# An RWKV-7 branch inside a two-layer trunk: per-layer state steps for all head pairs at once, small-tile matmul groups emitted whole, 64-row operands padded to 128 rows

## The chip, the cores and the metric

The kernel runs on one core of one Trainium2 chip. The metric is the device time of one execution in microseconds (us), less is better. Engines are named as the profile names them: PE is the matmul engine (TensorE), PEld its weight loads, DVE VectorE, ACT ScalarE, POOL GpSimd, SP SyncE, whose queue issues nearly all DMAs.

## The reference, cut to what matters

512 tokens of width 2048 go through two layers. Each layer normalises x, projects it with `w_in`, feeds three branches (an mLSTM with 4 heads, an attention with 8 heads, an RWKV-7 with 8 heads of 64), gates and concatenates them and projects back with `w_out`. The change lies in the RWKV branch:

```python
def rwkv7_scan(r, w, k, v, a_vec, b_vec):
    def step(S, inp):
        rt, wt, kt, vt, at, bt = inp
        sa = jnp.einsum('bhvk,bhk->bhv', S, at)
        S = S * wt[:, :, None, :] + sa[..., None] * bt[:, :, None, :] + vt[..., None] * kt[:, :, None, :]
        return S, jnp.einsum('bhvk,bhk->bhv', S, rt)
...
    log_w = -jax.nn.softplus(-(w0 + jnp.tanh(xw) @ w2)) - 0.5
    a = jax.nn.sigmoid(a0 + xa @ a2)
    if vres is None: v_first = v
    else: v = v + (v_first - v) * jax.nn.sigmoid(v0 + (v @ v1) @ v2)
    ...
    y = rwkv7_scan(r_h, heads(decay), k_h, v_h, -kk, kk * a_h)
    y = head_layer_norm(y, ln_g, ln_b, RW_GN_EPS)
    y = y + jnp.sum(r_h * k_h * r_k, axis=-1, keepdims=True) * v_h
```

## The kernel before

**The big products.** `gemm` computes 256 columns of `h @ w_in` per call, as 4 weight tiles of 512 KB. Each value is split into two fp32r parts, so a product is three passes (line 235; line 231 for `mv`, token-major). The outputs are called `pg_rk`, `pg_mq` and so on after the columns; all have 128 contracted rows and fill the whole array. Weight tiles come over SP as `raw_*` (lines 319, 324) and are split by ACT (`whi_*`, line 146) and DVE (`wlo_*`, line 147). Results are parked in DRAM and fetched again. `w_out` is the same in `out_products` (`po`, line 1347).

**The RWKV branch** is worked in chunks of 64 tokens, two heads (a pair) at a time on 128 partitions, 4 pairs a layer. `rw_pair(p)` is a generator that yields between its steps:

1. decay and gate: `psw`, `psa` (lines 710 to 714). Each adds a high part on 128 rows and a low part that lies in 64 rows of the tile `wal`.
2. keys: `kk`, `kh`, `bk` (on POOL, line 760), `ar`; then `psG` (line 773): per chunk and head one matmul with 64 rows, 128 columns of weights and 128 moving columns, for two heads in two banks, in two halves of 4 chunks.
3. `psTk` transposes (line 803), then the inverse of a 64x64 triangular matrix: 16x16 blocks on DVE between two DRAM round trips (`inv_d`), then 32x32 tiles on PE: `psQ`, `psT`, `psQ` again (`psQ64`), `psX` (lines 866, 887, 895).
4. `v` (with its correction in layer 1), its transposes, `psR` (line 798), `psW` (line 933, 64x64 tiles), then `psN` and `psY` (lines 798 and 954, 128 rows, 64 columns) and `psM` (line 933).
5. the state: for chunks 1 to 7 in turn, two `psY` matmuls that add to the output (line 960), two `psS` matmuls (line 964) and one DVE step that makes the next S (line 966).
6. norm over the heads, transposes `psTy`, gate, store to `mix_d`.

**What sets the order.** The program is written as generators that `bg.along(ratio, main, side, every)` interleaves: for each step of `main` it emits `ratio` steps of the big products, and every `every` steps one of `side`. Pairs 0 to 2 run their steps 5 and 6 beside steps 1 and 2 of the next pair; pair 3 runs them beside `ml_head(0)` and `ml_head(1)`. The compiled program is not in that order: the tile context places each engine's instructions by a simulated timeline, so that single matmuls of the big products land between small ones wherever a bank or an operand isn't ready. An fp32 matmul of the program is two records in the trace, an fp32r matmul one.

**Banks and buffers.** Two PSUM banks have the tag `bank`, two `bank2`, three `gbank` (big products), one `bank3`. `psG` and `prod2` took theirs from `bank` alone. The tag `tmp` has four buffers of 256 KB.

Of the kernel before, what the change touches and what calls it, by code (L numbers as in the profile page):

```python
# [12 lines left out]
F32 = mybir.dt.float32  # L13
# [9 lines left out]
T = 512  # L23
# [4 lines left out]
R_HEADS, R_ATT = 0.8, 0.0  # L28
# [45 lines left out]
def trunk(ctx, tc, a, out):  # L74
# [6 lines left out]
    dma = nc.sync.dma_start  # L81

# [430 lines left out]
    for l in range(DEPTH):  # L513
# [27 lines left out]
        def misc_out(u, ps, l=l):  # L541
            if u == 0:
                wa = stage(f"wa{l}")
                shift(wa, normed(stage(f"wn{l}"), ps), 12)
                act(wa[0:64], wa[0:64], AF.Tanh)

                kept["wa"] = whh, ahh, wal = [rp.tile([128, T], F32R, name=f"{n}{l}") for n in ("whh", "ahh", "wal")]
                for m, own in ((whh, slice(0, 64)), (ahh, slice(64, 128))):
                    for r in (0, 64):
                        act(m[r:r + 64], wa[own], AF.Copy)  # L550
                    tt(wal[own], wa[own], m[own].bitcast(F32), ALU.subtract)
                return
# [104 lines left out]
        xp_ctx = ExitStack()  # L657
        xp = xp_ctx.enter_context(tc.tile_pool(name=f"xp{l}", bufs=1, side="left"))
# [21 lines left out]
        def rw_pair(p, l=l):  # L680
# [4 lines left out]
            whh, ahh, wal = kept["wa"]  # L685

            tailp, tails, tbank = (xp, ("late", 3), bank2) if p < 3 else (rp, ("tmp", 4), bank)

            def late(name):
                return tailp.tile([128, T], F32, tag=tails[0], bufs=tails[1], name=f"{name}{nm}")  # L690
# [23 lines left out]
            mm(psa, lhsT=a2[64:128, sl], rhs=wal[64:128], start=False, stop=True)  # L714
# [38 lines left out]
            bv = tailp.tile([128, T], F32, tag="bv", bufs=2 if p < 3 else 1, name=f"bv{nm}")  # L753
            nc.scalar.copy(bv, ps)

            hs = [slice(0, 64), slice(64, 128)]
            bk = rp.tile([128, 8, 2, 64], F32, tag="bk", name=f"bk{nm}")
            for h, q in enumerate(hs):
                for slot, x in ((h, kk), (1 - h, kh)):
                    nc.gpsimd.tensor_tensor(bk[q, :, slot, :], x[q].rearrange(c64, t=64), Ei[q].rearrange(c64, t=64), ALU.mult)  # L760

            yield "keys"
            GG = rp.tile([128, 2, 8, 192], F32, tag="GG", name=f"GG{nm}")
            wide = tmp("wide").rearrange("p (c t) -> p c t", t=64)
            marb = mar.rearrange("p a t -> p (a t)")
            for half in range(2):
                cs = slice(half * 4, half * 4 + 4)
                pv = [bank(f"psG{half}{h}{nm}").rearrange("p (c n) -> p c n", n=128) for h in range(2)]  # L770
                for c in range(4):
                    for h, q in enumerate(hs):
                        mm(pv[h][:, c, :], lhsT=bk[q, half * 4 + c].rearrange("p s t -> p (s t)"),
                           rhs=ar[q, :, half * 4 + c, :], start=True, stop=True)
                for h in range(2):
                    tt(GG[:, h, cs, 0:128], pv[h], marb[:, None, :].broadcast_to([128, 4, 128]), ALU.mult)
                yield

            def token_major(blocks, dst, nn):

                ps = bank(f"psT{nn}{nm}")
# [11 lines left out]
            def prod(lhs, rhs, name):  # L793

                pv = bank(f"{name}{nm}").rearrange("p (c n) -> p c n", n=64)
                for c in range(8):
                    for h, q in enumerate(hs):
                        mm(pv[q, c, :], lhsT=lhs(h, c), rhs=rhs(h, c), start=True, stop=True)
                return pv
# [7 lines left out]
            yield  # L807

# [12 lines left out]
            both = small([64, 2, 512], "AR", "TX")  # L821
# [37 lines left out]
            flip()  # L859

# [11 lines left out]
            tt(Q, prod32(lambda q, c, n: GG[q, n // 2, c, n % 2 * 32:n % 2 * 32 + 32], blk(T32), "psQ"),  # L872
               mq.rearrange("p a b -> p (a b)")[:, None, :].broadcast_to([128, 8, 32]), ALU.mult)
# [15 lines left out]
            for h in range(2):  # L889
                nc.scalar.copy(Q[q4[2 * h + 1]], pv[q4[2 * h + 1]])  # L890
            ps = bank(f"psX64{nm}")
            pv = ps[:, 0:256].rearrange("p (c n) -> p c n", n=32)
            for c in range(8):
                for h in range(2):
                    mm(pv[q4[2 * h], c, :], lhsT=Q[q4[2 * h + 1], c, :], rhs=X32[q4[2 * h + 1], c, :],
                       start=True, stop=True)
# [5 lines left out]
            v = fetch("rv")  # L902
            if l > 0:
                bg.ensure("rv1")
                ps = bank(f"psv2_{nm}")
                mm(ps, lhsT=v2[:, p * 128:(p + 1) * 128], rhs=kept["vv"], start=True, stop=True)
                yield
                s = tmp("vs")
                sigm(s, ps, pch(R_V0 + p))
                vf = tmp("vf")  # L910
                dma(vf, vf_d[p])
                tt(vf, vf, v, ALU.subtract)
                tt(vf, vf, s, ALU.mult)
                tt(v, v, vf, ALU.add)
            tt(bv, bv, v, ALU.mult)

            UV = rp.tile([128, 2, 8, 64], F32, tag="UV", name=f"UV{nm}")
            token_major(lambda tb: v[:, tb * 128:(tb + 1) * 128], lambda h: UV[hs[1 - h], h], "v")
            yield
            AR = small([128, 8, 128], "AR")  # L920
            token_major(lambda tb: ar[:, 0, 2 * tb:2 * tb + 2, :].rearrange("p c n -> p (c n)"),
                        lambda h: AR[hs[h], :, 0:64], "a")
            nc.scalar.copy(AR[:, :, 64:128], prod(lambda h, c: GG[hs[1 - h], h, c, 0:64],
                                                  lambda h, c: UV[hs[1 - h], h, c, :], "psR"))
            yield

            def prod2(lhs, rhs, name):

                for half in range(2):
                    pv = bank(f"{name}{half}{nm}").rearrange("p (c n) -> p c n", n=128)  # L930
                    for c in range(4):
                        for h, q in enumerate(hs):
                            mm(pv[q, c, :], lhsT=lhs(h, half * 4 + c), rhs=rhs(h, half * 4 + c), start=True, stop=True)
                    yield slice(half * 4, half * 4 + 4), pv
            Wm = small([128, 8, 64], "Wm")
            for cs, pv in prod2(lambda h, c: X[hs[h], c, :], lambda h, c: AR[hs[h], c, :], "psW"):
# [3 lines left out]
                yield  # L940
            MT, Yl, DN = [late(n).rearrange("p (c n) -> p c n", n=64) for n in ("MT", "Yl", "DN")]
            dc = tailp.tile([128, 8], F32, tag="dc", bufs=2, name=f"dc{nm}")
            nc.vector.tensor_copy(dc, E[:, :, 64])
            tt(DN, prod(lambda h, c: GG[:, h, c, 128:192], lambda h, c: UV[:, h, c, :], "psN"),
               dc[:, :, None].broadcast_to([128, 8, 64]), ALU.mult)
            yield
            for cs, pv in prod2(lambda h, c: Wm[hs[h], c, :], lambda h, c: GG[hs[h], h, c, 64:192], "psM"):
# [3 lines left out]
            psY = tbank(f"psY{nm}").rearrange("p (c n) -> p c n", n=64)  # L951
            for c in range(8):
                for h, q in enumerate(hs):
                    mm(psY[q, c, :], lhsT=GG[:, h, c, 64:128], rhs=UV[:, h, c, :], start=(c == 0), stop=(c == 0),
                       skip_group_check=True)
            yield "state"
            S = DN[:, 0, :]
            for c in range(1, 8):
                for q in hs:
                    mm(psY[q, c, :], lhsT=Yl[q, c, :], rhs=S[q], start=False, stop=True, skip_group_check=True)  # L960
                if c < 7:
                    psS = tbank(f"psS{nm}_{c}")[:, 0:64]
                    for q in hs:
                        mm(psS[q], lhsT=MT[q, c, :], rhs=S[q], start=True, stop=True)
                    S2 = rp.tile([128, 64], F32, tag="S", bufs=2, name=f"S{nm}_{c}")
                    stt(S2, psS, dc[:, c:c + 1], DN[:, c, :], ALU.mult, ALU.add)
                    S = S2
                    if c % 2 == 0:
                        yield
            Y = late("Y").rearrange("p (c n) -> p c n", n=64)  # L970
            nc.scalar.copy(Y, psY)


            st = rp.tile([128, 2, 8], F32, tag="st", name=f"st{nm}")

            def c8(m):
                return m[:, :, None].broadcast_to([128, 8, 64])
            nc.vector.tensor_reduce(st[:, 0, :], Y, AX.X, ALU.add)
            tsc(st[:, 0, :], st[:, 0, :], 1.0 / 64, None, ALU.mult)
            tt(Y, Y, c8(st[:, 0, :]), ALU.subtract)  # L980
            sq = late("ysq")
# [516 lines left out]
```

## Time and profile before

| | |
|---|---|
| median of 3 runs | 2037.14 us (2032.81, 2037.14, 2037.67) |
| the profiled execution: time, span | 2034.48 us, 2032.8 us |
| mean granted PE clock | 0.997 of full |
| DVE busy | 1226.3 us (60%), 2127 instructions |
| ACT busy | 844.2 us (42%), 1435 instructions |
| DMA | 252.27 MB, 124 GB/s in the mean |

The span is the time from the first to the last instruction that the profiler saw; the time of the same execution is 1.7 us longer. A PE that is shown busy may still wait inside that time: matmul ends are modelled, so distances between starts say more than durations.

### The profile page before, as it was taken

The numbers are of one execution on the slowest core, as the hardware profiler recorded it, in microseconds if no ns is written. First come the engines' busy times: TensorE is split into PE (matmuls) and PEld (weight loads), VectorE is DVE, ScalarE is ACT, GpSimd is POOL, SyncE is SP. The second block draws the span as 40 slices with busy tenths as digits, with TensorE's granted clock in tenths as the row PEclk, the third lists the DMA queues.
The fourth block names the chain that finished last, engine by engine and source line by source line (L and its number), as shares of the span: only waits on it lengthen the run. The fifth ranks groups of instructions, "written<-read, shape, count | busy, mean of one in ns | idle before, by whom it ended". The sixth has DMA issues, their size and how long they took to land.

```text
span 2032.8 us, 31556 instructions
## 1 busy us (share of the span) xinstructions
PE 1998.6 (98%) x12544; PEld 1644.6 (81%) x12544; DVE 1226.3 (60%) x2127; ACT 844.2 (42%) x1435; POOL 137.2 (7%) x168
## 2 busy tenths in 40 slices
PE   8999999999999999999999999999999999899998
PEld 6887787888778888888888777877978888787886
DVE  6764766667646578633366547647657657885333
ACT  6523334244425446422263234234334445664223
POOL 3000101001000021000001001001010000210000
PEclk9999999999999999999999999999999999999999
DMA  5442443424445543344444333434424435533334
GB/s 170 140 125 86 118 120 99 120 84 133 116 128 161 169 117 97 114 145 132 131 114 137 110 109 105 120 104 119 125 75 137 142 118 172 147 113 121 121 118 155
DMA packets 239481, 252.27 MB, mean 124 GB/s; under 512 B 49204, under 2 KB 177406, under 8 KB 239334
## 3 DMA queue, kind: packets, MB, share of 16 engines
q1 hardware_dynamic: 238486, 249.29, 40.5%
q8 instruction: 98, 1.61, 0.3%
q0 software_dynamic: 848, 0.97, 0.2%
q14 instruction: 49, 0.40, 0.1%
HBM read 206.16 MB, written 44.06 MB: 123 GB/s over the span
## 4 chain that ended last, share of the span: by engine, by line
PE 91%; DVE 3%; DMA 2%; ACT 2%; issue 1%; SPq 0%; POOL 0%; ACTq 0%; DVEq 0%
PE po L1347 17%; PE pg_az L235 7%; PE pg_mv L231 5%; PE pg_rr L235 4%; PE pg_mq L235 4%; PE pg_rz L235 4%; PE pg_cq L235 4%; PE pg_mk L235 4%; PE pg_rk L235 4%; PE pg_rv L235 4%; PE pg_mo L235 4%; PE pg_mz L235 4%; PE pssc L1268 2%; PE pg_misc L235 2%; PE pg_ck L235 2%; PE psqn L1205 2%
## 5 line engine op out<-in xcount | busy, mean ns | idle before, releaser
L1347 PE MATMUL po<-whi_o,mh 128*128 128x512 f32 x512 | 200.3, 391 | 0.1
L1347 PE MATMUL po<-whi_o,ml 128*128 128x512 f32 x512 | 199.3, 389 | 0.0
L147 DVE TENSOR_TENSOR wlo_o<-raw_o,whi_o 128x1024 fp32r<-128x1024 f32 x64 | 78.3, 1225 | 188.6 <-ACT whi_o L146 187.4
L1347 PE MATMUL po<-wlo_o,mh 128*128 128x512 f32 x512 | 187.7, 390 | 0.0
L146 ACT ACTIVATE whi_o<-raw_o 128x1024 fp32r<-128x1024 f32 x64 | 67.7, 1059 | 204.2 <-PE po L1347 168.6
L1347 PEld LDWEIGHTS po<-whi_o,mh 128*128 128x128 f32 x512 | 96.2, 188 | 20.4 <-DVE Vl L250 0.6
L1347 PEld LDWEIGHTS po<-wlo_o,mh 128*128 128x128 f32 x512 | 96.0, 188 | 20.0
L1347 PEld LDWEIGHTS po<-whi_o,ml 128*128 128x128 f32 x512 | 96.1, 188 | 19.6
L235 PE MATMUL pg_az<-xl,whi_az 128*128 128x512 f32 x256 | 100.8, 394 | 0.0
L235 PE MATMUL pg_az<-xh,whi_az 128*128 128x512 f32 x256 | 100.8, 394 | 0.0
L235 PE MATMUL pg_az<-xh,wlo_az 128*128 128x512 f32 x256 | 100.0, 394 | 0.0
L760 POOL TENSOR_TENSOR bk<-kk,Ei 64x512 f32<-64x512 f32 x16 | 25.8, 1614 | 817.2 <-DVE E L721 476.0
L231 PE MATMUL pg_mv<-whi_mv,xl 128*128 128x256 f32 x256 | 73.2, 286 | 0.0
L231 PE MATMUL pg_mv<-whi_mv,xh 128*128 128x256 f32 x256 | 73.0, 285 | 0.0
L231 PE MATMUL pg_mv<-wlo_mv,xh 128*128 128x256 f32 x256 | 72.7, 285 | 0.0
L235 PEld LDWEIGHTS pg_az<-xl,whi_az 128*128 128x128 f32 x256 | 48.1, 188 | 9.5
L235 PEld LDWEIGHTS pg_az<-xh,wlo_az 128*128 128x128 f32 x256 | 48.1, 188 | 9.3
L235 PEld LDWEIGHTS pg_az<-xh,whi_az 128*128 128x128 f32 x256 | 48.1, 188 | 9.2
L147 DVE TENSOR_TENSOR wlo_az<-raw_az,whi_az 128x1024 fp32r<-128x1024 f32 x32 | 39.1, 1222 | 26.4 <-ACT whi_az L146 26.4
L235 PE MATMUL pg_rk<-xh,whi_rk 128*128 128x512 f32 x128 | 50.7, 400 | 1.4 <-ACT xh L248 1.4
L235 PE MATMUL pg_rk<-xl,whi_rk 128*128 128x512 f32 x128 | 51.6, 404 | 0.0
L235 PE MATMUL pg_mz<-xl,whi_mz 128*128 128x512 f32 x128 | 51.4, 401 | 0.0
(564 smaller groups left out, 5606.3 us busy)
## 6 DMA issues: line engine op xcount, KB each, us to landing
raw_o<-in_w_out_dram SPq DMA_DIRECT2D x64, 512.0 KB
raw_az<-in_w_in_dram SPq DMA_DIRECT2D x32, 512.0 KB
raw_rk<-in_w_in_dram SPq DMA_DIRECT2D x16, 512.0 KB
raw_rr<-in_w_in_dram SPq DMA_DIRECT2D x16, 512.0 KB
raw_rv<-in_w_in_dram SPq DMA_DIRECT2D x16, 512.0 KB
raw_rz<-in_w_in_dram SPq DMA_DIRECT2D x16, 512.0 KB
raw_mq<-in_w_in_dram SPq DMA_DIRECT2D x16, 512.0 KB
raw_mk<-in_w_in_dram SPq DMA_DIRECT2D x16, 512.0 KB
```

What stands on the lines that cost most here:

```text
L146: act(hi, raw, AF.Copy)
L147: (nc.gpsimd if name[0] == "u" or name in ("misc0_0", "misc0_1") else nc.vector).tensor_tensor(lo, raw, hi.bitcast(F32), ALU.subtract)
L231: mm(ps[u][:, (tb % 2) * 256:(tb % 2) * 256 + 256], lhsT=xx[:, sl], rhs=w[:, i, :], start=(k == 0 and n == 0 and tb % 2 == 0), stop=(k == ...
L235: mm(ps[u], lhsT=w[:, i, u * 128:(u + 1) * 128], rhs=xx, start=(k == 0 and n == 0), stop=(k == 15 and n == 2))
L760: nc.gpsimd.tensor_tensor(bk[q, :, slot, :], x[q].rearrange(c64, t=64), Ei[q].rearrange(c64, t=64), ALU.mult)
L1205: mm(ps, lhsT=w[:, i, :], rhs=xx, start=(i == 0 and j == 0), stop=(i == n - 1 and j == 2))
L1268: mm(ps[:, 0:n], lhsT=x1[:, ts_], rhs=x2[:, 0:n], start=(j == 0), stop=(j == 5))
L1347: mm(pss[tb], lhsT=xx[:, sl], rhs=w, start=(k == korder[0] and j == 0), stop=(k == korder[15] and j == 2))
```

## The change

It computes the same. The order on PE, the banks and the tiles change:

- `misc_out`: the low parts get tiles of their own, `wl` and `al`, whose other 64 rows are zeros, so the second matmul of `psw` and `psa` has 128 rows.
- `in_order()` marks PE instructions that the placing keeps in the written order.
- `rw_pair`: `v` and its transposes come before `psG`; the four `psG` banks are taken at once (two `bank`, two `bank2`) and heads alternate; `psR` follows `psQ`; `psW` and `psM` use both tags; `psM`, `psN`, `psY` are one group. `psY` holds only the part inside a chunk and goes to `Y0`. `MT`, `DN`, `dc` go to tiles for all pairs; `bv`, `Y0`, `Yl` are written to DRAM (`tail_d`).
- `rw_states`: after all four pairs, six steps of 8 matmuls and two DVE instructions for all pairs; then per pair three loads from `tail_d`, 14 matmuls `psYl` and the norm as before, with scale and bias in the four ACT copies out of `psTy`.
- the driver: pairs one after another, one step of the big products per step; then `rw_states` beside `ml_head(0)`, `ml_head(1)`.

```diff
-R_HEADS, R_ATT = 0.8, 0.0
+R_PAIRS, R_HEADS, R_ATT = 1.0, 0.8, 0.0
...
+    def in_order():
+
+        return tc.manual_schedule(engines={mybir.EngineType.PE})
...
-                    tt(wal[own], wa[own], m[own].bitcast(F32), ALU.subtract)
+                    tt(lo[own], wa[own], m[own].bitcast(F32), ALU.subtract)
+                    tsc(lo[other], wa[own], 0.0, None, ALU.mult)
...
-            mm(ps, lhsT=w2[0:64, sl], rhs=wal[0:64], start=False, stop=True)
+            mm(ps, lhsT=w2[:, sl], rhs=wl, start=False, stop=True)
...
-            for half in range(2):
-                cs = slice(half * 4, half * 4 + 4)
-                pv = [bank(f"psG{half}{h}{nm}").rearrange("p (c n) -> p c n", n=128) for h in range(2)]
-                for c in range(4):
-                    for h, q in enumerate(hs):
-                        mm(pv[h][:, c, :], lhsT=bk[q, half * 4 + c].rearrange("p s t -> p (s t)"),
-                           rhs=ar[q, :, half * 4 + c, :], start=True, stop=True)
...
+            pv = [[(bank, bank2)[half](f"psG{half}{h}{nm}").rearrange("p (c n) -> p c n", n=128) for h in range(2)]
+                  for half in range(2)]
+            with in_order():
                 for c in range(8):
+                    for h in (1, 0):
+                        mm(pv[c // 4][h][:, c % 4, :], lhsT=bk[hs[h], c].rearrange("p s t -> p (s t)"),
+                           rhs=ar[hs[h], :, c, :], start=True, stop=True)
...
+                pv = [bank_(f"{name}{half}{nm}").rearrange("p (c n) -> p c n", n=128)
+                      for half, bank_ in enumerate((bank, bank2))]
+                with in_order():
+                    for c in (4, 5, 6, 7, 0, 1, 2, 3):
+                        for h in (1, 0):
+                            mm(pv[c // 4][hs[h], c % 4, :], lhsT=lhs(h, c), rhs=rhs(h, c), start=True, stop=True)
...
+            with in_order():
+                M = prod2(lambda h, c: Wm[hs[h], c, :], lambda h, c: GG[hs[h], h, c, 64:192], "psM")
+                psN = prod(lambda h, c: GG[:, h, c, 128:192], lambda h, c: UV[:, h, c, :], "psN")
+                psY = prod(lambda h, c: GG[:, h, c, 64:128], lambda h, c: UV[:, h, c, :], "psY", bank2)
...
+            dma(tail_d[p, 1].rearrange("p (c n) -> p c n", n=64), Y0)
+            dma(tail_d[p, 2].rearrange("p (c n) -> p c n", n=64), Yl)
...
+        def rw_states(l=l):
+            for c in range(1, 7):
+                psS = bank(f"psS{l}_{c}")[:, 0:256].rearrange("p (a n) -> p a n", n=64)
+                for p in range(4):
+                    for q in hs:
+                        mm(psS[q, p, :], lhsT=MTa[q, p, c, :], rhs=DNa[q, c - 1, p, :], start=True, stop=True)
+                S = tp.tile([128, 4, 64], F32, tag="S", bufs=2, name=f"S{l}_{c}")
+                tt(S, psS, dca[:, :, c:c + 1].broadcast_to([128, 4, 64]), ALU.mult)
+                tt(DNa[:, c], DNa[:, c], S, ALU.add)
                 yield
...
+                for i, t in enumerate((bv, Y, Yl)):
+                    dma(t, tail_d[p, i])
...
+                for c in range(1, 8):
                     for q in hs:
+                        mm(psY[q, c, :], lhsT=Yl[q, c, :], rhs=DNa[q, c - 1, p, :], start=True, stop=True)
+                tt(Y[:, 1:8, :], Y[:, 1:8, :], psY[:, 1:8, :], ALU.add)
...
-        pairs = [rw_pair(p) for p in range(4)]
         for p in range(4):
-            bg.along(R_HEADS, upto(pairs[p], "state"))
-            if p < 3:
-                bg.along(R_HEADS, pairs[p], (upto(pairs[p + 1], "keys"),), 1)
+            bg.along(R_PAIRS, rw_pair(p))
+        rp_ctx.close()
         xp_ctx.close()
+        tp = sp_ctx.enter_context(tc.tile_pool(name=f"tp{l}", bufs=1, side="right"))
...
-        bg.along(R_HEADS, pairs[3], (ml_head(0), ml_head(1)))
+        bg.along(R_HEADS, rw_states(), (ml_head(0), ml_head(1)))
```

**The order that comes out.** In the compiled program PE has 10820 matmuls before and after. First the place of `psG`, layer 0, pair 1. A name ends in the layer or pair and a buffer number, so each `psG_1_...` is one bank; an `x4` stands for four matmuls in a row. Before, on PE:

```order
L235 MATMUL pg_mq_2729<-xl_14_162,whi_mq_3_2900 128x512
L773 MATMUL psG_1_1806<-ar_1_1719,bk_1_1786 128x128 x4
L773 MATMUL psG_1_1817<-ar_1_1719,bk_1_1786 128x128 x4
L235 MATMUL pg_mq_2729<-xh_14_146,wlo_mq_3_2901 128x512
L235 MATMUL pg_mq_2729<-xh_15_147,whi_mq_3_2900 128x512
```

and in the change:

```order
L817 MATMUL psG_1_1857<-ar_1_1764,bk_1_1811 128x128
L239 MATMUL pg_mq_2512<-xl_7_155,whi_mq_1_2516 128x512
L239 MATMUL pg_mq_2512<-xh_7_139,wlo_mq_1_2517 128x512
L817 MATMUL psG_1_1856<-ar_1_1764,bk_1_1811 128x128
L817 MATMUL psG_1_1857<-ar_1_1764,bk_1_1811 128x128
L817 MATMUL psG_1_1856<-ar_1_1764,bk_1_1811 128x128
L817 MATMUL psG_1_1857<-ar_1_1764,bk_1_1811 128x128
```

Before, the 16 matmuls of a pair stand in three places (4, then these 8, then 4) with the heads in blocks of four; in the change one stands alone and 15 follow in a row, heads alternating (8 more rows of this kind follow).

Second the state steps of layer 0. Before, on PE, chunk 3 of pair 0:

```order
L235 MATMUL pg_rv_2355<-xh_1_133,wlo_rv_0_2282 128x512
L960 MATMUL psY_0_1539<-S_0_2_1580,Yl_0_1465 64x64 x2
L964 MATMUL psS_0_3_1614<-S_0_2_1580,MT_0_1464 64x64 x2
L705 MATMUL psn_1_1664<-psnx_1_1661,bones 128x512
L235 MATMUL pg_rv_2355<-xh_2_134,whi_rv_0_2281 128x512
```

and in the change chunk 2 of all pairs:

```order
L239 MATMUL pg_mo_5195<-xl_4_152,whi_mo_1_5198 128x512
L978 MATMUL psS_2_3999<-DN_587,MT_586 64x64 x8
L239 MATMUL pg_mo_5195<-xh_4_136,wlo_mo_1_5199 128x512
L239 MATMUL pg_mo_5195<-xh_5_137,whi_mo_1_5198 128x512
L239 MATMUL pg_mo_5195<-xl_5_153,whi_mo_1_5198 128x512
```

What stood in 24 places a layer with two matmuls each stands in 6 or 7 with 8. `psYl` follows pair by pair, 14 matmuls in a row.

Third SP's queue at the start of `rw_states`, layer 0, in the change:

```order
L1053 DMA mv_0_4045<-mv_d_130 128x4x128
L990 DMA bv_0_4241<-tail_d_589 128x512
L990 DMA Y_0_4242<-tail_d_589 128x512
L990 DMA Yl_0_4243<-tail_d_589 128x512
L993 DMA sz_0_4247<-park_d_129 128x512
L990 DMA bv_1_4335<-tail_d_589 128x512
L990 DMA Y_1_4336<-tail_d_589 128x512
L990 DMA Yl_1_4337<-tail_d_589 128x512
L993 DMA sz_1_4341<-park_d_129 128x512
L323 DMA raw_mz_0_5256<-in_w_in_dram 128x4x256
```

Before, `raw_mz_1` followed `mv_0` at once; now eight loads of 256 KB stand between the loads of `ml_head(0)` (`nb`, `mq`, `mk`, `mv`) and the next weight tile.

Counted over both compiled programs, the stretches in which PE works with small tiles, between two stretches of full 128x128 tiles, are 164 before and 94 after; the changes from one small shape to another inside them 40 and 16. The trace of before has the same 164 and 40. Of the 164, 25 hold `psG`, of the 94, 15. Between a pair's last `psG` and its `psQ`, the change has 23.8 us of PE work in pair 1 of layer 0 at the durations of the trace, and more in every other pair.

## Rows read from the trace of the kernel before

**Rows 1.** The profile's first part: span; busy time, share, instructions.

```profile
span 2032.8 us, 31556 instructions
PE 1998.6 (98%) x12544; PEld 1644.6 (81%) x12544; DVE 1226.3 (60%) x2127; ACT 844.2 (42%) x1435; POOL 137.2 (7%) x168
```

**Rows 2.** Stretches: from:to, length, busy per engine, clock, DMA share, GB/s (RWKV stages).

```profile
60.00:510.00 450.00, 450.00 (x3250) 368.90 (x3250) 294.45 (x440) 174.50 (x244) 30.70 (x20) 1.00 0.39 114
1140.00:1600.00 460.00, 459.12 (x3450) 373.88 (x3449) 274.94 (x430) 169.70 (x249) 23.01 (x15) 1.00 0.39 114
```

**Rows 3.** Waits of PE, the longest: us in total, times, longest.

```profile
PE psHT L1081 <- DVE hn L1077: 4.2, 1, 4.2
```

**Rows 4.** Timeline of PE: start us, us, instruction, count. One state step.

```profile
206.90 0.39 PE L235 MATMUL pg_rv<-xh,wlo_rv 128*128 128x512 f32 x1
207.22 0.33 PE L960 MATMUL psY<-S,Yl 64*64 64x64 f32 x4
207.38 0.28 PE L964 MATMUL psS<-S,MT 64*64 64x64 f32 x4
207.60 0.50 PE L235 MATMUL pg_rv<-xh,whi_rv 128*128 128x512 f32 x1
207.94 0.39 PE L235 MATMUL pg_rv<-xl,whi_rv 128*128 128x512 f32 x1
```

**Rows 5.** Timeline of PE: the three places of psG of one pair.

```profile
238.33 1.16 PE L773 MATMUL psG<-ar,bk 64*128 64x128 f32 x8
239.42 0.50 PE L235 MATMUL pg_mq<-xl,whi_mq 128*128 128x512 f32 x1
...
244.33 0.39 PE L235 MATMUL pg_mq<-xh,whi_mq 128*128 128x512 f32 x1
244.56 0.39 PE L235 MATMUL pg_mq<-xl,whi_mq 128*128 128x512 f32 x1
244.88 1.71 PE L773 MATMUL psG<-ar,bk 64*128 64x128 f32 x16
246.52 0.50 PE L235 MATMUL pg_mq<-xh,wlo_mq 128*128 128x512 f32 x1
246.85 0.39 PE L235 MATMUL pg_mq<-xh,whi_mq 128*128 128x512 f32 x1
...
251.07 1.16 PE L773 MATMUL psG<-ar,bk 64*128 64x128 f32 x8
252.15 0.66 PE L803 MATMUL psTk<-idf,bk 128*128 128x128 f32 x4
```

**Rows 6.** Timeline of PE: psW of the same pair.

```profile
300.34 1.96 PE L933 MATMUL psW<-AR,X 64*64 64x128 f32 x32
302.24 0.39 PE L231 MATMUL pg_mv<-whi_mv,xl 128*128 128x256 f32 x1
```

**Rows 7.** Timeline of PE: psM between psN and psY.

```profile
306.09 1.09 PE L933 MATMUL psM<-GG,Wm 64*64 64x128 f32 x16
307.11 0.91 PE L954 MATMUL psY<-UV,GG 128*64 128x64 f32 x22
307.95 1.09 PE L933 MATMUL psM<-GG,Wm 64*64 64x128 f32 x16
```

**Rows 8.** Groups by shape on DVE: busy us, mean ns: the copies out of psG.

```profile
L776 DVE TENSOR_TENSOR GG<-psG,mar 128x512 f32<-128x512 f32 x32 | 21.5, 687 | 4.9 <-PE psG L773 4.6
```

**Rows 9.** DMA queue: packets, MB, share of 16 engines.

```profile
q1 hardware_dynamic: 238486, 249.29, 40.5%
```

**Rows 10.** Tile raw_mq: ns min/median/max, first and last start; then the chain of waits.

```profile
L319 SPq DMA_DIRECT2D raw_mq<-in_w_in_dram x16: 367/380/449, 208.1 to 1391.1; - x16
225.72 12.24 PE pg_mq L235 x53
```

**Rows 11.** Timeline: the last step of the inverse on DVE, and psQ on PE.

```profile
277.97 0.44 DVE L858 STREAM_TRANSPOSE X<-T 128x256 f32<-128x256 f32 x1
278.73 0.75 PE L866 MATMUL psQ<-T,GG 32*32 32x32 f32 x64
```

More of the change, by code (lines that the diff above doesn't have):

```diff
@@ L684, in tmp @@
                 return rp.tile([128, T], F32, tag="tmp", bufs=4, name=f"{name}{nm}")
[L685 to L690, printed above, removed]
+            whh, ahh, wl, al_ = kept["wa"]
             def fetch(kind):
@@ L807, in rw_pair, with prod @@
             yield
+            def prod(lhs, rhs, name, bank_=bank):
+                pv = bank_(f"{name}{nm}").rearrange("p (c n) -> p c n", n=64)
+                for c in range(8):
+                    for h, q in enumerate(hs):
+                        mm(pv[q, c, :], lhsT=lhs(h, c), rhs=rhs(h, c), start=True, stop=True)
+                return pv
             def small(shape, tag, name=None):
@@ L820, in rw_pair @@
             dma(A16, inv_d[0].rearrange("c a s t -> (c a) s t"))
-            both = small([64, 2, 512], "AR", "TX")
+            both = small([64, 2, 512], "TX")
             pr = both[:, 1, :]
@@ L859, in rw_pair @@
             flip()
+            for _ in range(3):
+                yield
             def prod32(lhs, rhs, name):
@@ L893, in rw_pair @@
             for c in range(8):
-                for h in range(2):
+                for h in (1, 0):
                     mm(pv[q4[2 * h], c, :], lhsT=Q[q4[2 * h + 1], c, :], rhs=X32[q4[2 * h + 1], c, :],
@@ L899, in rw_pair @@
             yield
[L902 to L925, printed above, removed]
-            def prod2(lhs, rhs, name):
[L929 to L934, printed above, removed]
+            def prod2(lhs, rhs, name):
+                pv = [bank_(f"{name}{half}{nm}").rearrange("p (c n) -> p c n", n=128)
+                      for half, bank_ in enumerate((bank, bank2))]
+                with in_order():
+                    for c in (4, 5, 6, 7, 0, 1, 2, 3):
+                        for h in (1, 0):
+                            mm(pv[c // 4][hs[h], c % 4, :], lhsT=lhs(h, c), rhs=rhs(h, c), start=True, stop=True)
+                return [(slice(half * 4, half * 4 + 4), pv[half]) for half in range(2)]
             Wm = small([128, 8, 64], "Wm")
@@ L948, in rw_pair @@
+            nc.scalar.copy(Y0, psY)
+            for cs, pv in M:
                 tt(Yl[:, cs, :], pv[:, :, 0:64], ar[:, 1, cs, :], ALU.add)
                 tt(MT[:, cs, :], pv[:, :, 64:128], i64[:, None, :].broadcast_to([128, 4, 64]), ALU.add)
-                yield
[L951 to L962, printed above, removed]
-                    for q in hs:
[L964 to L981, printed above, removed]
-            act(sq, Y.rearrange("p c n -> p (c n)"), AF.Square)
```

144 lines of the change are left out of this document (95 added, 49 removed).

## The prediction

> **What bounds the kernel now.** I read four views in this order. First the shares: PE is busy for 1998.6 of 2032.8 us, DVE for 60% and ACT for 42% [rows 1]. A PE that is called busy may still lose time, so next the stretches of the two RWKV stages: in 450 and 460 us PE is idle for 0.0 and 0.9 us, DVE is busy for two thirds, and the DMA engines for 0.39 [rows 2]; the clock column says 1.00 of full, that is the 2.4 GHz level. Nothing but PE's own list of work ends last there. Third the waits of PE: the longest is one of 4.2 us, a transpose of `ml_head` that waits for DVE [rows 3]. Fourth the timeline, where starts tell what the durations hide. A full-size matmul of the big products starts 0.23 us after the one before it. Around a state step that spacing breaks: start to start, the step from 206.90 to 207.22 is 0.32 us, and 207.60 to 207.94 is 0.34 us, 0.09 and 0.11 us too much, though PE waits for nobody [rows 4]. So the chip takes a toll for each visit to a small tile shape and each return, and the change is about the number of visits and about how densely small matmuls are packed inside one.
>
> **The prices.** One visit: from 206.90 to 207.94 are 1.04 us; two full-size steps of it are 0.46, leaving 0.58 us for 8 records of 64x64 tiles [rows 4]. What such records cost when packed I take from the block of 22 in 0.84 us [rows 7]: about 0.03 each after the block's own start, 0.24 for 8. The visit's toll is then 0.34 us. A change of shape inside a visit: `psM` takes 1.02 us for 16 records [rows 7], and `psW`, with the same shape, 1.90 us for 32 [rows 6]. From the two, a record costs 0.055 and a block has 0.14 to 0.15 us on top: 0.15 us a change.
>
> **Term 1, psG.** Now a pair pays 1.09, 1.64 and 1.08 us, and at each place the two borders, 0.09 to enter (244.56 to 244.88) and 0.10 to leave (246.52 to 246.85) [rows 5]: 3.81 + 3 x 0.19 = 4.4 us. After the change it is one block of 32 records with the heads alternating. What that costs is the only disputed price of the sum. Lower bound: `psW`, where the two heads use different row halves and alternate, 1.90 us for 32 [rows 6]. Upper bound: no overlap, four blocks of eight at 1.09 less three starts of 0.19, 3.8 us [rows 5]. I take 1.92, near the lower bound, because the 16-record place shows the overlap with `psG` itself: it holds a block of one head and then one of the other, and needs 1.64 us where two places of 8 need 2.17 [rows 5]; one saved start is 0.19, the other 0.34 us can only be matmuls of the two heads that ran at once near the seam. So 4.4 - (1.92 + 0.19) = 2.3 us a pair, 18.2 us for eight. In seven of eight pairs the new order leaves one `psG` matmul alone ahead of the rest, a visit more: 7 x 0.37 = 2.6 us back. Term 1 is 15.6 us, with 0.6 us as its lower and 18.2 us as its upper end.
>
> **Term 2, the other visits.** 164 - 25 = 139 now, 94 - 15 = 79 then: 60 fewer. They are the 16 low parts of `psw` and `psa`, some 34 state places, and about 10 where `psN`, `psM` and `psY` were torn apart. 60 x 0.34 = 20.4 us. The padded low parts cost no matmul time: both widths stream 512 columns.
>
> **Term 3, changes of shape inside visits.** 40 to 16: 24 x 0.15 = 3.6 us. Sum of the three: 39.6 us of PE's own time.
>
> **What the change adds.** DVE gets 28 instructions fewer in all and longer ones (a state step for four pairs replaces four of 0.28 us); the norm's scale moves to ACT. Both have a third of the RWKV stage and more to spare [rows 2], so I cost them at nothing; what covers them is the big products, of which both orders have enough until the last `az` tile. The 48 DMAs of `tail_d` add 12.6 MB to 252; q1 moves 249.29 MB in 40.5% of the span [rows 9], so they cost 5% of a resource at 0.4, nothing while weights come in time. On SP eight loads now stand ahead of a weight tile at the start of `rw_states`; rival 2 prices that.
>
> **New waits.** Two things get less cover. The inverse: today `psQ` starts 26.6 us after the pair's last `psG` block, and its operand was ready 0.3 us before (277.97 + 0.44 against 278.73) [rows 5, 11]; the change gives 23.8 us in that pair. At worst 2.8 us are lost there, at best none, as DVE then has less from the neighbouring pair in its queue. And in layer 1 the last `ml_head` falls behind the last big product, so attention's first matmuls must cover it; its nearest price is the 4.2 us wait [rows 3], which may itself go away. Together I take 3 us lost, with bounds of -4 (a gain) and +20.
>
> A rule of the Trainium skill speaks against term 1. Its page TensorEngine Tiling (Array Packing), section Restrictions and Gotchas, says that row tiling raises PSUM pressure, since different row tiles write to different banks. Here four banks are held at once instead of two, and the next user, `psTk`, has 9 full matmuls or 2.0 us ahead of it; DVE empties a bank in 0.69 us, four in 2.75 [rows 8]. By the rule at its worst PE would wait 0.7 us a pair, 5.6 us in all, and the sum would be 34 us; but the half that `psTk` needs is complete 1 us before the other and is emptied first, so I leave the term out.
>
> **The sum.** 39.6 - 3 = 36.6 us off the profiled execution's 2034.5 us gives 1998 us. That execution is 2.7 us faster than the median of the three runs; against the median the same gain would be 2000.5, and I stay with 1998.
>
> **The rivals.**
>
> 1. *The halves do not overlap in `psG`.* It has 64x128 tiles, so both heads feed all 128 columns, unlike `psW`, whose heads have their own columns too. For it: no place in the trace alternates them one by one. Against: the 0.34 us at the seam. Term 1 falls to 0.6 us, the gain to 24.6 - 3: 2013 us.
>
> 2. *The weights come late.* Twelve loads of 256 KB, 3.1 MB, are issued in a row before the next weight tile, in each layer. At the rate of the page (249.29 MB in 0.405 x 2032.8 us, 303 GB/s) they take 10.4 us [rows 9]. Against it: a weight tile is issued 17.6 us before its first matmul (208.1 to 225.72) [rows 10]. The rival holds where the loads must also wait for memory that the last pair frees. 5 to 10 us a layer, perhaps with the waits above: 2005 to 2020, 2013 as its centre.
>
> 3. *Slower: the inverse ends last.* Pairs no longer overlap, so while DVE and two DRAM round trips make the inverse there is nothing but big products to run, and PE keeps its order: if the chain is longer than the 23.8 to 33 us of work that stand there, PE stands still. It decides from 39.6 / 8 = 5 us more per pair: a chain of some 30 us instead of 26.6. At 6 us a pair PE loses 48 us: 2034.5 - 39.6 + 48 = 2043. For it: `psQ` had only 0.3 us to spare [rows 11]. Against: that slack came from where it was placed, and the change moves work out of DVE's queue there, not into it.
>
> 4. *The order is not kept or the toll isn't PE's.* If the borders were only how starts are recorded, fewer visits would give nothing: 2034 us. Against it: no time is left over in 450 us of unbroken PE work [rows 2], so each 0.1 us that is shown is a 0.1 us in which no product advanced.
>
> **How the numbers follow.** Chances: the forecast 0.66, rival 1 0.09, rival 2 0.18, rival 3 0.04, rival 4 0.03. The forecast's own range is 1988 (all of term 1, the 4.2 us wait gone) to 2006. To leave out no more than 2 in 10 the range takes in the centres of rivals 1 and 2 and some of their upper halves: 1988 to 2017. A measurement of this kernel can tell about 0.3%, 6 us, from no change; faster means under 2031 us. The forecast and rivals 1 and 2 are all faster: 0.93. The same: rival 4, 0.03. Slower: rival 3, 0.04.
>
> **What would show it.** In the new profile the `psG` block should be 31 or 32 records in about 1.9 us, with no start later than 0.12 us after the one before it; 3.6 us would mean rival 1. `psS` should come 16 records at a time with borders of 0.09 and 0.11 us. `psw` and `psa` should have 0.23 us spacing. PE's waits in the RWKV stages should stay within a few us; waits of `pg_mz` or `pg_cq` for `whi_*` would show rival 2, waits of `psQ` for the transposed `X` or `T` rival 3. The forecast is wrong if the spans of small matmuls shrink as said and the time does not, or if they don't shrink.

## The result, and the profile after

The change takes 2009.86 us in the median (four runs, 2009.12 to 2010.58), before takes 2036.93 (four runs beside it): a ratio of 0.9871, 95% interval 0.9854 to 0.9888. The forecast was 1998 us with a range of 1988 to 2017. So the sign and the range were right, though the forecast's own range, 1988 to 2006, ended below the result. Of the 36.6 us that were summed up against the profiled execution, 27 came by the medians and 23.9 by the two profiled spans (2032.8 and 2008.9 us). All ledgers below are made with the profiled spans.

The shares alone don't show what is missing. The page of the change, first part (span; busy time, share and count of each engine), answers to [rows 1]:

```profile
span 2008.9 us, 31622 instructions
PE 1968.0 (98%) x12544; PEld 1636.9 (81%) x12544; DVE 1221.6 (61%) x2099; ACT 842.1 (42%) x1439; POOL 135.3 (7%) x168
```

PE is again busy for 98%. The prices of the prediction, too, stand in the trace as they were said. Timeline of PE in the change (start us, us, instruction, count), answering to [rows 5], [rows 4] and the low parts; psG of pair 1 of layer 0, a state step, and a pair's psw:

```profile
224.88 0.49 PE L817 MATMUL psG<-ar,bk 64*128 64x128 f32 x2
225.29 0.50 PE L239 MATMUL pg_mq<-xl,whi_mq 128*128 128x512 f32 x1
225.63 0.40 PE L239 MATMUL pg_mq<-xh,wlo_mq 128*128 128x512 f32 x1
225.96 2.05 PE L817 MATMUL psG<-ar,bk 64*128 64x128 f32 x30
227.93 0.50 PE L239 MATMUL pg_mq<-xh,whi_mq 128*128 128x512 f32 x1
...
477.77 0.39 PE L239 MATMUL pg_mo<-xl,whi_mo 128*128 128x512 f32 x1
478.08 0.68 PE L978 MATMUL psS<-DN,MT 64*64 64x64 f32 x16
478.70 0.50 PE L239 MATMUL pg_mo<-xh,wlo_mo 128*128 128x512 f32 x1
479.04 0.39 PE L239 MATMUL pg_mo<-xh,whi_mo 128*128 128x512 f32 x1
...
190.18 0.40 PE L719 MATMUL psw<-whh,w 128*128 128x512 f32 x1
190.41 0.40 PE L720 MATMUL psw<-wl,w 128*128 128x512 f32 x1
190.65 0.39 PE L239 MATMUL pg_rr<-xh,wlo_rr 128*128 128x512 f32 x1
```

Read the starts. The block of 30 psG records takes 1.97 us to the next start, where three places took 3.8 [rows 5]. A state step of 16 records takes 0.62 us (478.08 to 478.70), with 0.08 us too much ahead of it (477.77 to 478.08 is 0.31) and 0.11 behind it. The padded low part starts 0.23 us after the high part and the next product 0.24 us after it: no toll is left.

Where, then, did 13 us go? The view that answers it is the first and last start of a tile, in layer 1 (engine op out<-in xcount: duration ns min/median/max, first to last start; forms). Before:

```profile
L235 PE MATMUL pg_az<-xh,wlo_az x128: 387/389/485, 1608.5 to 1727.9; 128*128 128x512 f32 x128
L1081 PE MATMUL psHT<-idf,hn x16: 270/272/328, 1592.0 to 1729.1; 128*128 128x128 f32 x16
L1205 PE MATMUL pskn<-ckh,wlo_uqk x16: 388/393/397, 1737.2 to 1832.1; 128*128 128x512 f32 x16
```

and in the change:

```profile
L239 PE MATMUL pg_az<-xh,wlo_az x128: 387/389/486, 1575.5 to 1683.2; 128*128 128x512 f32 x128
L1113 PE MATMUL psHT<-idf,hn x16: 270/272/421, 1582.3 to 1723.5; 128*128 128x128 f32 x16
L1231 PE MATMUL pskn<-ckh,wlo_uqk x16: 388/393/628, 1694.0 to 1808.0; 128*128 128x512 f32 x16
```

`pg_az` is the last big product, `psHT` the last step of the heads on PE, `pskn` a product of attention, the first one at its start, the last one 26 us before attention's last matmul on PE (`pso`, 1834.1 us in the change). Before, the last `psHT` came 1 us behind the last `pg_az`. In the change the big products are done 44.7 us earlier and the heads 5.6 us: `psHT` ends 40 us behind them. The way from the last `pg_az` to the last `pskn` grew from 104.2 to 124.8 us. In layer 0 of the change the same rows give 704.9 for `pg_az`, 676.0 for `psHT` and 805.1 for `pskn`, 100.2 us (99.8 before): there the heads are done first.

The ledger, from starts of such rows: layer 0, first to last big product, 714.1 to 693.8 us, 20.3 won. Layer 1, 705.2 to 680.3, 24.9 won. Attention's start in layer 1, 20.6 lost. All else within 0.5 us. The sum is 24 us, so layer 0 kept its whole gain and layer 1 kept 4 us.

What the 20.6 us are shows in the 62 us behind the last big product of layer 1 (from:to, length, busy per engine, clock, DMA share, GB/s), before, then the change:

```profile
1728.00:1790.00 62.00, 56.10 (x320) 46.26 (x319) 53.72 (x120) 40.86 (x88) 16.32 (x10) 1.00 0.44 129
```

```profile
1683.00:1745.00 62.00, 48.98 (x234) 39.97 (x233) 46.19 (x94) 37.34 (x74) 13.01 (x9) 0.83 0.39 116
```

PE does 234 records instead of 320. It idles for 13.0 us instead of 5.9, and the granted clock is 0.83 instead of 1.00, so for a third of the stretch it stood at the 1.2 GHz level. By the starts of PE's records from the last `pg_az` to the last `pskn`, the 20.6 us are 5.5 of head matmuls that only moved there (30 `psN` and 9 `psSm` records), 7.0 of longer waits (13.2 instead of 6.2) and 8.1 of matmuls that took longer. And the waits of PE there have new names. The longest of them in the change (1683 to 1745 us; us in total, times, longest), answering to [rows 3]:

```profile
PE pskn L1231 <- DVE Vl L254: 4.4, 1, 4.4
PE psqn L1231 <- ACT whi_uqk L150: 2.0, 1, 2.0
PE psN L1082 <- ACT meh L252: 1.9, 1, 1.9
PE psqn L1231 <- DVE knl L254: 1.4, 1, 1.4
```

The wait of 4.2 us of `psHT` [rows 3], which lay in layer 0 (at 528 us), is gone, as half expected; 4.4 us came in attention of layer 1. What this wait hangs on stands in the chain of work that ended last (start us, us, what; steps of under 0.15 us left out):

```profile
1723.08 0.84 PE psHT L1113 x4
1723.95 0.76 DVE go L1119
1724.73 1.97 DMA mix_d<-go
1726.81 0.61 ACT Vh L252
1727.44 0.70 DVE Vl L254
1728.27 2.90 PE pskn L1231 x6
```

The last `psHT` gives the output of the last head, a DMA stores it, and only then ACT, which had been idle for 6.4 us, writes `Vh` of attention: in the kernel the pool of `Vh` is opened when the pool of the heads is closed.

### The profile page after: what moved, and what is told of

It is laid out like the page before. It is cut to its first block, busy times and chain, and to the rows that moved or that the text cites. A ratio compares the mean times of both kernels' runs of the same rounds, so it can differ in the third digit from the quotient of the medians.

```text
span 2008.9 us, 31622 instructions
## 1 busy us (share of the span) xinstructions
PE 1968.0 (98%) x12544; PEld 1636.9 (81%) x12544; DVE 1221.6 (61%) x2099; ACT 842.1 (42%) x1439; POOL 135.3 (7%) x168
## 3 DMA queue, kind: packets, MB, share of 16 engines
q1 hardware_dynamic: 245398, 261.88, 42.7%
## 4 chain that ended last, share of the span: by engine, by line
PE 86%; DVE 6%; DMA 4%; ACT 2%; issue 2%; SPq 0%; ACTq 0%; DVEq 0%
PE po L1373 17%; PE pg_az L239 6%; PE pg_mz L239 4%; PE pg_cq L239 4%; PE pg_rr L239 4%; PE pg_rz L239 4%; PE pg_rv L239 4%; PE pg_mv L235 4%; PE pg_mo L239 4%; PE pg_rk L239 4%; PE pg_mq L239 3%; PE pg_mk L239 3%; PE pssc L1294 2%; PE pg_ck L239 2%; PE pg_misc L239 2%
## 5 line engine op out<-in xcount | busy, mean ns | idle before, releaser
L1373 PEld LDWEIGHTS po<-whi_o,mh 128*128 128x128 f32 x512 | 96.1, 188 | 20.6 <-DVE Vl L254 0.6
L1373 PEld LDWEIGHTS po<-wlo_o,mh 128*128 128x128 f32 x512 | 96.0, 188 | 19.9
L1373 PEld LDWEIGHTS po<-whi_o,ml 128*128 128x128 f32 x512 | 96.1, 188 | 19.6
L239 PE MATMUL pg_mo<-xl,whi_mo 128*128 128x512 f32 x128 | 50.6, 395 | 0.0
```

The source lines that it names most:

```text
L239: mm(ps[u], lhsT=w[:, i, u * 128:(u + 1) * 128], rhs=xx, start=(k == 0 and n == 0), stop=(k == 15 and n == 2))
L1373: mm(pss[tb], lhsT=xx[:, sl], rhs=w, start=(k == korder[0] and j == 0), stop=(k == korder[15] and j == 2))
```

## The experiments

**The theories.** A: in layer 1 the end isn't set by PE's work but by a chain: four pairs one after another, then four heads one after another (each needs the buffers of the one before it), then attention, which needs the heads out of the way. It grew, because pairs no longer overlap (from the first big product of layer 1 to the last `psHT` 706.4 us before, 720.6 in the change), while PE's work shrank; so what PE saves in layer 1 turns into waits. B: attention's start waits for its own weights and transfers, or PE's saving is smaller than summed; then it doesn't matter when the heads end.

**e1: a shorter chain in layer 1.** Two edits that leave every matmul as it is. (As with every edit, the tile context then places the rest of the program anew, so a few microseconds can come or go by that alone.) First, `v`'s correction and transposes move behind `psTk`:

```diff
-            v = fetch("rv")
-            if l > 0:
-                bg.ensure("rv1")
...
+            late_v = l > 0
+            if not late_v:
+                UV = yield from v_part()
...
+            if late_v:
+                yield
+                UV = yield from v_part()
             def prod(lhs, rhs, name, bank_=bank):
```

Second, the first step of the next pair is written while a pair makes its inverse (and `dc` is copied as soon as `E` is there, in both layers; in layer 0 first to last big product stays at 694.3 us, 693.8 in the change):

```diff
+            if l in (1,) and p < 3:
+                bg.along(R_PAIRS, upto(pairs[p], "mid"))
+                bg.along(R_PAIRS, upto(pairs[p + 1], "decay"))
+            bg.along(R_PAIRS, pairs[p])
```

> The edit touches layer 1 alone: v's correction and its transposes stand after psTk instead of ahead of psG, and a pair's psw, psa and decay are written while the pair before it makes its inverse. Matmuls are the same. Theory A (in layer 1 the chain of pairs and then heads ends last, 40 us after the last big product, and attention's start waits for it): the last psHT comes before or within 10 us of the last pg_az, the stretch from the last pg_az to the last pskn shrinks from 124.8 us to the 100 of layer 0, of which 5 us return as matmuls of ml_head(3) ahead of the last pg_az; time 1990 us (1986 to 1997), and the stretch 1710 to 1730 has no clock of 0.68. Theory B (attention's start waits for its own weights or transfers, or the lost 13 us lie elsewhere on PE): 2007 to 2011 us.

Measured: 2000.88 us, ratio to before 0.9827 (0.9813 to 0.9840). The last `psHT` stands at 1687.0, 10.8 us ahead of the last `pg_az` at 1697.8, and the way from there to the last `pskn` is 101.5 us: that part of A came out within 2 us. But first to last big product took 694.7 us, 14.4 more than in the change, not 5. The waits of PE in that stage (1500 to 1700 us) say in part why:

```profile
PE psrck L1178 <- ACT cksq L1173: 1.9, 1, 1.9
PE psSm L1078 <- DVE me L1085: 1.3, 1, 1.3
PE pg_az L239 <- DVE wlo_az L151: 0.8, 1, 0.8
```

With the heads done early, the first reductions of attention (`psrck`) stand further ahead among the `pg_az` (305 rows before the last one, 230 in e2), and PE, which works its list in order, stood before them. Behind that wait the granted clock was 0.50 (1631 to 1634 us), and eight `pg_az` started 0.43 us apart. Of the 9 us beyond the 5 that were said, waits are 4.2 and the slower steps some 1.5 (an estimate from these starts); the rest stays open. Of the 15 us that new waits and slower matmuls had cost, 9 came back.

**e2: the first edit alone.**

> Half the dose of the run before: only v's correction and transposes move behind psTk in layer 1. Theory A: the last psHT of layer 1 comes 20 to 30 us after the last pg_az instead of 40; time 1998 to 2006 us, between the change and the run with both edits. Theory B: 2007 to 2011 us.

Measured: 1996.35 us, 0.9809 (0.9795 to 0.9822), 1.7 us below A's range, and in the median 4.5 us below e1, though the intervals of the two overlap. Last `psHT` 1712.8, last `pg_az` 1691.9, last `pskn` 1796.3: the lag fell from 40 to 21 us, the way to the last `pskn` from 124.8 to 104.4.

**e5: the second edit alone.**

> The other half of e1 alone, in layer 1: psw, psa and decay of a pair are written while the pair before it makes its inverse; v stays ahead of psG. In the compiled order the last psHT of layer 1 stands 81 rows behind the last pg_az (the change 139, e2 71). Theory A (any edit that shortens the chain of layer 1 gives the same): the last psHT 20 to 25 us behind the last pg_az, 1997 us (1994 to 2002). If e2 gained by what was done to v and not by the shorter chain: 2007 to 2011 us.

Measured: 1997.67 us, 0.9815 (0.9802 to 0.9828); last `psHT` 1711.0, last `pg_az` 1690.9, last `pskn` 1794.5. Two edits with nothing in common but the length of the chain give the same time within 1.4 us, and the same lag of 20 to 21 us.

**e8: the first edit, in layer 0 alone** (`late_v = l == 0`).

> The edit of e2 in layer 0 alone, nothing in layer 1. Theory A: in layer 0 the heads end 29 us ahead of the last pg_az, so a shorter chain is worth nothing there: 2010 us (2008 to 2012). If v behind psTk is worth something by itself (fewer waits around psG and psQ), half of what e2 gained: 2001 to 2005 us.

Measured: 2008.96 us, 0.9866 (0.9853 to 0.9880): nothing, as A says. The edit is worth 13.5 us where the chain ends last and less than 1 us where PE does.

**e3 and e4: one undo, in layer 0 and in layer 1.** The heads of `psG` in blocks, the low parts on 64 rows:

```diff
+            lo64, hi64 = (slice(0, 64), slice(64, 128)) if l == 0 else (slice(0, 128),) * 2
+            mm(ps, lhsT=w2[lo64, sl], rhs=wl[lo64], start=False, stop=True)
...
-                for c in range(8):
-                    for h in (1, 0):
+                for c, h in ([(c, h) for h in (1, 0) for c in range(8)] if l == 0 else
+                             [(c, h) for c in range(8) for h in (1, 0)]):
```

> Undone in layer 0 alone: the heads of psG come as two blocks of eight (still one order, four banks), and the low parts of psw and psa read 64 rows again. By the prices of the prediction: 8 visits at 0.34 to 0.39 us, 3 us; psG from 2.4 us to 3.4 to 3.6 us a pair, 4 to 5 us. Where PE ends last, as in layer 0 by both theories, the time rises by 7 to 8 us, to 2017 us (2014 to 2019). If the heads did not overlap in psG, or the toll were none, 2010 us.

> The same undone in layer 1 alone. Theory A: PE's own 7 to 8 us in layer 1 only push the last big product towards the end of the heads' chain, and the waits behind it shrink by as much: 2010 us (2007 to 2013). Theory B (PE's own time counts in layer 1 as in layer 0): 2017 us (2014 to 2019).

Measured: layer 0 2012.22 us, 0.9887 (0.9873 to 0.9900); layer 1 2007.30 us, 0.9860 (0.9846 to 0.9873). In layer 1 the undo costs nothing, as A says (in the median it is even 2.6 us faster: in the profiled execution the last `psHT` came 5 us earlier, at 1718.5, and the lag was 21 us; why the chain got shorter stays open). In layer 0 it costs 2.4 us where 7 to 8 were said, a miss. Both intervals overlap with that of the change (0.9854 to 0.9888), so these two times alone decide little; the traces and e9 say more. The prices are there (timeline of PE in e3, pair 1 of layer 0):

```profile
191.53 0.40 PE L719 MATMUL psw<-whh,w 128*128 128x512 f32 x1
191.86 0.49 PE L721 MATMUL psw<-wl,w 64*128 64x512 f32 x1
192.28 0.50 PE L239 MATMUL pg_rr<-xl,whi_rr 128*128 128x512 f32 x1
...
227.96 3.50 PE L818 MATMUL psG<-ar,bk 64*128 64x128 f32 x32
231.38 0.50 PE L239 MATMUL pg_mq<-xl,whi_mq 128*128 128x512 f32 x1
```

A `psG` group with the heads in two blocks takes 3.42 us (227.96 to 231.38) against 0.41 + 1.97 with the heads alternating, and a 64-row low part costs 0.33 + 0.42 us for two matmuls that take 0.23 each in the change. By the starts of their records `psG`, `psw` and `psa` take 6.4 us more in layer 0, but first to last big product grew by 4.1: the waits of PE between 100 and 690 us are 3.5 us in the change (`pg_mv` 1.1, `psT` 1.0, `psSm` 0.7 the longest) and 1.7 in e3. So even in layer 0 a saving is paid back in part, where PE's list had covered a wait. Behind the big products, attention's start in layer 0 is 1.3 us shorter than in the change (98.9 against 100.2 us to the last `pskn`).

**e6: a dose between e2 and e1** (e2, with the overlap for pair 3 alone: `p in (2,)`).

> e2 with the overlap for pair 3 alone: in the compiled order the last psHT of layer 1 stands 8 rows ahead of the last pg_az, between e2 (71 behind) and e1 (50 ahead), and the first psrck of attention 250 rows ahead of it (e1 305, e2 230). If e1 was slower than e2 because matmuls of attention's low-rank part and of the heads stand so early in PE's order that PE waits there: few of these waits, 1994 us (1991 to 1998). If every microsecond of lead costs: 1998 to 2000 us.

Measured: 1994.31 us (four runs, 1993.21 to 1994.50), 0.9795 (0.9782 to 0.9808). It beats before and the change; the intervals don't touch. Its rows of layer 1, and the 62 us behind the last big product:

```profile
L239 PE MATMUL pg_az<-xh,wlo_az x128: 387/389/479, 1581.8 to 1692.3; 128*128 128x512 f32 x128
L1123 PE MATMUL psHT<-idf,hn x16: 270/271/328, 1564.8 to 1691.1; 128*128 128x128 f32 x16
L1251 PE MATMUL pskn<-ckh,wlo_uqk x16: 388/390/393, 1699.5 to 1791.7; 128*128 128x512 f32 x16
```

```profile
1692.00:1754.00 62.00, 58.11 (x330) 48.49 (x329) 55.42 (x120) 37.75 (x86) 18.32 (x11) 1.00 0.42 124
```

The heads end with the big products, as they did before the change; idle time is 3.9 us, the clock 1.00 again, and the way to the last `pskn` 99.4 us. Of e1's waits none is left: between 1500 and 1695 us the view lists no wait of PE at all.

**e9: e4's undo on e6.**

> The undo of e4 (heads of psG in blocks of eight, low parts on 64 rows, layer 1 alone) on the kernel of e6, where the heads' chain no longer ends behind the last pg_az. In e4 these two edits lengthened the small shapes of layer 1 by 6.3 us in psG and 2.2 us in psw and psa, and the time did not rise. Theory A: with the chain out of the way PE ends last in layer 1 too, and the same undo costs what it takes: 6 to 9 us, 2000 to 2003 us. If PE's time in layer 1 never counts: 1994 us (1992 to 1996).

Measured: 2007.59 us, 0.9863 (0.9846 to 0.9879), 13.3 us more than e6. The same undo that was free behind a late chain costs time as soon as PE ends last: A's sign. The last `psHT` stayed where it was (1692.1, in e6 1691.1), the last `pg_az` moved from 1692.3 to 1705.6. The size is above what was said: first to last big product grew by 15.5 us, of which `psG`, `psw` and `psa` are 8.6 by the starts of their records, and 2.0 are waits of `pg_az` for DVE's `wlo_az`, as in e1. Another 2.8 are longer steps of the big products: here the undo brought 12 more visits to small shapes in layer 1 (61 instead of 49), as the `psG` stand in 12 places instead of 8; in e4 it brought 8. The last 2 us stay open.

Put side by side, the runs give one curve for layer 1: with the last `psHT` 40 us behind the last `pg_az` (the change, e3, e8) the way from there to the last `pskn` takes 125 us; with 20 to 21 us (e2, e4, e5) 104 to 105; with the heads done first (e1, e6, e9) 99 to 102, as in layer 0. Before, with 1 us, it took 104. (e7, below, has another chain.) So attention's start covered some 20 us of lag almost for nothing, and the next 20 us cost 20. That is the strongest evidence for A, and B has no place for it; only the wait of 2.0 us of `psqn` for its weights `whi_uqk` in the change (0.6 before) is of B's kind.

**e7: state steps pair by pair, on e2.**

```diff
-            for c in range(1, 7):
-                psS = bank(f"psS{l}_{c}")[:, 0:256].rearrange("p (a n) -> p a n", n=64)
+            for P in ([(0, 1, 2, 3)] if l not in (0, 1) else [(0,), (1,), (2,), (3,)]):
...
+                for c in range(1, 7):
```

> e2 with the state steps pair by pair in both layers, in 48 steps of 2 matmuls instead of 12 of 8: 120 visits to small shapes instead of 94, the same matmuls. Toll of 0.34 us a visit: 26 visits, 8.8 us, of which those in layer 1 (4.4) may be taken back by shorter waits at attention's start; 2001 to 2005 us. If the visits cost nothing: 1995 to 1998 us.

Measured: 2027.95 us, 0.9964 (0.9951 to 0.9976), 31.6 us more than e2, a miss of 23. The toll is as said; a step of 4 records (timeline of PE in e7):

```profile
477.00 0.39 PE L239 MATMUL pg_mo<-xh,whi_mo 128*128 128x512 f32 x1
477.31 0.33 PE L988 MATMUL psS<-DN,MT 64*64 64x64 f32 x4
477.58 0.50 PE L239 MATMUL pg_mo<-xl,whi_mo 128*128 128x512 f32 x1
477.91 0.39 PE L239 MATMUL pg_mo<-xh,wlo_mo 128*128 128x512 f32 x1
```

0.27 us for a quarter of the records that take 0.62 in the change, with the same borders: four such steps cost 4 x (0.27 + 0.19) = 1.84 us, one packed step 0.62 + 0.19 = 0.81, so each of the three saved visits is worth 0.34 us. By the starts of all records `psS` and the steps of the big products take 4.5 us more in layer 0 and 4.4 in layer 1, for 13 more visits in each: 0.34 again. First to last big product grew by only 2.0 us and 0.7, as some waits got shorter in layer 0 and 3.3 us of attention's reductions moved behind the last `pg_az` in layer 1. The loss is a second chain. 24 steps after one another last from 1529 to 1640 us; the last norm's transpose `psTy` comes at 1695.1; attention's tiles lie where the states' tiles lay, so its first loads (`ckr`) follow, the last at 1703.3. In e2 these two stand at 1626.4 and 1634.6 us, 8 us apart as here. Waits of PE in e7, and 35 us behind the last big product:

```profile
PE psrck L1168 <- ACT cksq L1163: 13.1, 2, 12.3
PE psqr L1241 <- ACT cqh L252: 3.9, 2, 3.5
...
PE psrb L1177 <- DVE rw L1174: 2.7, 1, 2.7
```

```profile
1690.00:1725.00 35.00, 15.63 (x65) 13.22 (x64) 19.03 (x28) 15.18 (x24) 2.77 (x2) 0.66 0.33 110
```

PE is busy for 15.6 of 35 us, and the clock falls to 0.66. So packing the states is worth more to the chain of layer 1 than to PE.

## Why the prediction was right, and where it was wrong

**What bounds the kernel: right for layer 0, not for layer 1.** "Nothing but PE's own list of work ends last there" was read from stretches in which PE is never idle [rows 2]. They are full in both layers, but in layer 1 they are full because the big products just last until the heads are done: 1727.9 against 1729.1 us. A full PE told how busy it was, not what would end last with less to do. The two last starts would have told it, and they weren't read.

**Terms 1 to 3: right in the sum.** By the starts of its records, with waits taken out, PE's own time from the first to the last big product fell by 19.9 us in layer 0, and in layer 1 by 23.8 less the 5.5 of head matmuls that only moved: 38 us, said 39.6. Term 1 alone was a little too large. By the starts of all records `psG` fell from 30.7 to 19.6 us; 10 places less, at 0.19, make it 13 us, said 15.6. The split-off matmul costs 0.41 us and its borders, not 0.37, and one wait of 0.3 us came in. What is left for the other two terms is 25 us, said 24. The choice near the lower bound was right: e3 measures 3.42 us for the blocks against 1.97. (The 0.19 us that the working took as a block's own start is the sum of the two outer borders; its own price for a start was 0.14 to 0.15. It would have put 0.04 us more on the overlap at the seam and changes nothing.)

**New waits: the step that failed.** "Together I take 3 us lost, with bounds of -4 (a gain) and +20." It cost 20.6 less 5.5, about 15 us. The place was named rightly ("in layer 1 the last `ml_head` falls behind the last big product, so attention's first matmuls must cover it"), but it was priced by one wait of 4.2 us, and that one lay in layer 0. It isn't one wait. The chain is late by 40 us; attention's start covers some 20 of it, and the rest falls into eleven waits of 0.2 to 4.4 us (7.0 us more than before); among them the clock fell (0.83), and what PE does there took 8.1 us longer. What cut the cover had been described but not priced: pairs one after another. In layer 1 pair 0 also waits for all of `rv`, since `v` now stands ahead of `psG`: its `psG` begins at 1148 us, 145 us after the layer's first product, before at 1106, 83 us after it. e2 moves just that: its `psG` begins 83 us after the first product again, and it gains 13.5 us.

**The cover: "enough until the last `az` tile"** held in layer 0 (28.9 us to spare) and not in layer 1.

**The range: held by luck.** The 15 us lie within the bounds of -4 and +20, but the forecast's own range didn't carry them: it ended at 2006, where a loss of 20 gives 2034.5 - 39.6 + 20 = 2015. The result lies inside 1988 to 2017 only because the centres of rivals 1 and 2 had been taken in, and neither of them came.

**PSUM pressure.** The rule of the Trainium skill (TensorEngine Tiling (Array Packing), section Restrictions and Gotchas) that row tiling raises PSUM pressure was left out of the sum, and rightly: `psTk` waits nowhere for its banks, and the one wait that four banks at once brought is 0.33 us at 416 us, `psG` of pair 3 of layer 0 behind ACT's copy out of `psTa`. At its worst 5.6 us had been worked out.

**The rivals.** Rival 1 (halves don't overlap): no, 1.97 us. Rival 2 (late weights): 2013 us was near the result, but for another reason; no wait of `pg_mz` or `pg_cq` for `whi_*` is in the trace, and q1 moves 261.88 MB in 42.7%. Rival 3 (inverse last): `psQ` waits 0.4 us in all and `psT` 1.0. Rival 4: no. What came was none of the four: a chain ends last, but the one from the pairs to attention, not the inverse.

## What to carry to other kernels

When work is taken off a full engine, look up for each stage when the next longest chain ends, by the last starts of its tiles. If they lie within a few microseconds, as here in layer 1, a saving is kept only as far as the next stage can cover the late chain (some 20 us here); beyond that it turns into waits until the chain is shortened too. Two short tests tell it: undo the saving where the suspected chain ends last (free, e4) and where the engine does (13 us, e9; in e3 it was too small to be clear of the noise); and shorten the chain without touching the engine's work (e2, e5). A chain that ends too early isn't free either (e1): an engine that works in order can meet the next stage's work before its inputs are there.

## What the runs showed that was not expected

- The toll of small shapes lies at both borders and inside. Entering a visit stretches the last full-size step from 0.23 to 0.32 us; leaving it adds 0.11; and a visit's own records take 0.14 us more than in a packed block. The Trainium skill (TensorEngine Tiling (Array Packing), section Tiling Modes) says that a change of the tiling mode drains the engine; the trace shows a price at both changes of a visit, which fits that, and its number is 0.34 us a visit.
- Heads that use different row halves overlap even with all 128 columns: a record of 64x128 starts 0.11 us after the one before it in a block of one head (3.42 us for 32) and two start together when the heads alternate (1.97 us for 30).
- The clock isn't only a matter of the start of a program. Twelve matmuls of attention in the change, just behind a wait of 1.44 us, start 0.43 us apart, nearly twice the usual step, four of them here:

```profile
1717.60 0.80 PE L1231 MATMUL psqn<-cqh,whi_uqk 128*128 128x512 f32 x1 [1.44 <-DVE knl L254]
1718.19 0.63 PE L1231 MATMUL psqn<-cql,whi_uqk 128*128 128x512 f32 x1
1718.62 0.63 PE L1231 MATMUL psqn<-cqh,wlo_uqk 128*128 128x512 f32 x1
1719.04 0.63 PE L1231 MATMUL psqn<-cqh,whi_uqk 128*128 128x512 f32 x1
```

  That is the 1.2 GHz level (granted clock 0.50 from 1717.6 to 1722.6 us), after a stretch with several waits; in the same place before the change PE idled 5.9 us of 62 and kept 1.00. So waits there cost more than their length: 7.0 us more of them came with 8.1 us of slower matmuls.
